# The first sample's inputs modulated in PSUM in a hybrid encoder, with new numbers for its order of work

## The chip, the cores and the metric

The kernel runs on one core of a Trainium2 chip. The metric is the device time of one execution in microseconds (us), as the median of several runs. A profile is taken in one further execution; its time is given beside its span, which goes from the first to the last instruction.

## What is computed

Two sequences of 1024 rows and 1024 columns, each with a conditioning vector, go through two layers with shared weights. For a layer:

```python
shift, scale, gate = jnp.split(jax.nn.silu(c) @ ada_w + ada_b, 3, axis=-1)
h = rmsnorm(x, norm_pre) * (1.0 + scale) + shift
u = h @ w_in                                  # 1024 x 2304
y_pool = pool_mixer(u[..., :256], ...)        # four windows
y_attn = gqa_attention(u[..., 256:1024], ...) # q, k, v; 8 heads of 64, 2 for k and v
y_rg = rglru_mixer(u[..., 1024:1280], ...)    # convolution, two linear recurrences
y = concatenate([y_pool, y_attn, y_rg]) * silu(u[..., 1280:])
x = x + gate * rmsnorm(y @ w_out, norm_post)
```

All inputs are fp32. To keep that precision the kernel splits each operand of a large product into two fp16 halves, hi and lo = value - hi, and adds up three products: hi*hi, hi*lo and lo*hi.

## The kernel before

There are four units of work, called samples 0 to 3: sample 0 is the prompt in layer 0, sample 1 the other sequence in layer 0, samples 2 and 3 the same in layer 1. Each has a stage that makes the transposed input hT (hi and lo, in two halves j of 512 rows and eight slices k of 128 columns), projections for k and v and for q, a side stream of chunks (recurrence, gate, pooling), attention in 64 units of 128 queries of one head, and the output projection (wout) in eight tiles of 128 rows.

At the beginning the modulation has to be computed as well: blocks of ada_w (adaw) are loaded, 24 in all, of which the first 16 give shift and scale; from these come the columns hgb that hT is multiplied with and shifted by. Sample 0's inputs (xt, eight blocks of 128 rows) are loaded and scaled by their row factor rs (norm, L849), four of them are transposed together per slice into a PSUM bank (turn, L862), and the result goes to xT in SBUF. If hgb is known by then, this eviction modulates; if not, it copies, and modulate (L885) does it later. modulate then writes hi, and lo is subtracted on DVE or POOL (sub_any). For samples 1 to 3 hprep_gen (L911) does the same with the bank itself as the buffer: modulate in place, copy to hi, subtract on DVE, free the bank.

The order of the instructions is not written by hand. A planner (class Order) keeps many streams of work, each of which says what it needs next: an engine, tiles, free slots of the pool of 39, PSUM banks. At each step it takes the stream that can go first by its own estimates, and among those that can go at the same time the one with the lowest rank. `soonest` puts an operation on the engine that would end it first. Every engine and the queue of DMA issues (SP) then run their lists in that order, so an instruction waits for all that stand before it on its engine.

The numbers come from four dictionaries TUNE (one a sample), START and LAYER: ranks (a stream of sample n has the rank 100 n plus its number), how far ahead of an engine a stream may be placed (P, A, D, G, S, X), how many PSUM banks may be held singly (nb) and in pairs (np), how many slots are left free by a stream (spare, qkeep, wkeep), how many tiles of wout take the eight inputs y one by one (f_major), from which chunk the next layer's w_out is prepared (wfrom). START["x"] says after how many adaw blocks the two halves of xt may be loaded; the adaw stream itself has the rank -97 (start_gen), these loads START["xr"], that is -53.8 and 1.4. TUNE[0]["h"] is the rank of h_gen for sample 0, which only starts h0_gen with START["h"].

Of the kernel before, what the change touches and what calls it, by code (L numbers as in the profile page):

```python
# [12 lines left out]
AF = mybir.ActivationFunctionType  # L13
# [3 lines left out]
P = 128  # L17
# [10 lines left out]


TUNE = [  # L30
    dict(h=-9.8, tab=-61.5, rgw=-62.8, qw=11.3, q=39.5, main=39.6, v=-93.1, rgt=6.2, attn=13.3,
         wprep=16.5, wo=39.7, side=108.5, gate=1.45, ysc=107.7, ysp=100.7, w=68.8, work=8, ds=3, nfly=8,
         s0=4, pace=(4, 61), wos=8, deep=3, f_major=5, spare=0, qkeep=1, wkeep=7, wokeep=0, slack=2.19,
         hslack=2.0, margin=0.33, P=0.6, A=1.22, D=1.02, G=1.25, S=1.3, X=2.99, nb=4, np=2, wopen=3,
         spill=2, sslack=0.0),
    dict(h=-88.0, tab=-138.2, rgw=-45.0, qw=-61.2, q=-181.1, main=65.6, v=-122.9, rgt=23.6, attn=-14.4,
         wprep=107.1, wo=85.3, side=97.8, gate=1.86, ysc=66.7, ysp=108.8, w=79.4, work=8, ds=2, nfly=5,
         s0=0, pace=(14, 64), wos=10, deep=3, f_major=6, spare=1, qkeep=5, wkeep=2, wokeep=9, slack=3.75,
         hslack=3.82, margin=0, P=0.07, A=1.29, D=0.36, G=1.39, S=1.66, X=1.74, nb=4, np=3, wopen=4,
         spill=2, sslack=0.0),  # L40
    dict(h=-56.5, tab=-120.9, rgw=-43.7, qw=-41.0, q=-17.5, main=-3.7, v=-95.2, rgt=51.8, attn=-16.0,
         wprep=71.4, wo=90.7, side=118.4, gate=0.1, ysc=142.5, ysp=110.2, w=62.9, work=6, ds=2, nfly=6,
         s0=3, pace=(15, 38), wos=9, deep=2, f_major=1, spare=4, qkeep=2, wkeep=0, wokeep=1, slack=2.33,
         hslack=2.48, margin=0.36, P=2.36, A=1.02, D=0.83, G=0.625, S=0.35, X=1.72, nb=6, np=2, wopen=3,
         spill=2, sslack=0),
    dict(h=-38.8, tab=-7.4, rgw=44.8, qw=-59.1, q=43.0, main=31.5, v=86.0, rgt=62.7, attn=36.1,
         wprep=226.9, wo=-31.1, side=118.1, gate=0.51, ysc=119.3, ysp=81.6, w=57.1, work=10, ds=3, nfly=5,
         s0=5, pace=(0, 64), wos=9, deep=4, f_major=3, spare=1, qkeep=5, wkeep=1, wokeep=0, slack=2.26,
         hslack=2.98, margin=0.87, P=0.28, A=0.15, D=0.45, G=0.9, S=1.99, X=0, nb=4, np=3, wopen=4,
         spill=2, sslack=0.28),  # L50
]
START = dict(x=(6, 16), xr=(-53.8009657012761, 1.4378218455368525), h=11.7, qw=-116.3, qw2=-141.6, qwa=9,
             prt=7, crow=4, prow=2, ada=95.9, keep=0)
LAYER = [
    dict(fly=6, keep=3, wfly=4, wfrom=(0, 0), wrank=15.7, ada=-17.0, akeep=5),
    dict(fly=3, keep=2, wfly=1, wfrom=(1, 1), wrank=163.6, ada=69.7, akeep=8),
]
LAT = {
    "P": dict(P=0.0, A=0.197, D=0.196, G=0.2, S=0.2), "A": dict(P=0.06, A=0.14, D=0.14, G=0.06, S=0.14),
# [253 lines left out]
def tile_hymba_encoder(  # L313
# [515 lines left out]
    def h0_gen(rank):  # L829
# [19 lines left out]
        def norm(j, xs, t):  # L849
            ss, rs = small(1, "ss"), small(1, "rs")  # L850
            yield need("A", [xs[t]])
            act(junk, xs[t], AF.Square, accum=ss)
            yield need("G", [ss])
            ts(rs, ss, 1.0 / D, EPS, ALU.mult, ALU.add, "G")
            tt(rs, rs, neghalf[:, :1], ALU.pow, "G")
            yield need("D", [rs])
            ts(xs[t], xs[t], rs, None, ALU.mult)
            done[j] = done.get(j, 0) + 1
            if done[j] == 4:
                yield from turn(j, xs)  # L860

        def turn(j, xs):  # L862
# [3 lines left out]
            for k in range(NK):  # L866
# [3 lines left out]
                    tp(ps[:, t * P:(t + 1) * P], xs[t][:, k * P:(k + 1) * P], ident)  # L870
                yield need("A|D", [ps])
                if ("hgb", 0) in G:
                    done["h", j, k] = True
                    g, b = (G["hgb", 0][:, i, k, 0:1] for i in range(2))
                    if soonest(("D", 0.66), ("A", 0.66)) == "D":
                        ts(xT[j, k], ps, g, b, ALU.mult, ALU.add)
                    else:
                        act(xT[j, k], ps, AF.Identity, scale=g, bias=b)
                else:
                    copy_any(xT[j, k], ps)  # L880
                free(ps)
                spawn(rank - 0.1 + 0.01 * k, modulate(j, k))
            free(*xs)

        def modulate(j, k):  # L885
            x = xT[j, k]
            hi, lo = hT(0, j, k)
            yield need("A|D", lambda: [x, G["hgb", 0]], cond=lambda: ("hgb", 0) in G)
            if ("h", j, k) in done:
                copy_any(hi, x)  # L890
            else:
                g, b = (G["hgb", 0][:, i, k, 0:1] for i in range(2))
                if soonest(("D", 0.46), ("A", 0.7)) == "D":
                    ts(hi, x, g, b, ALU.mult, ALU.add)
                else:
                    act(hi, x, AF.Identity, scale=g, bias=b)
                yield need("D", [x])
                ts(x, x, g, b, ALU.mult, ALU.add)
            yield need("D|G", [x, hi])
            sub_any(lo, x, hi, TUNE[0]["hslack"])  # L900
            G["hk", 0, j, k] = od.mark(f"hk0_{j}_{k}", hi, lo)
            done["m", j] = done.get(("m", j), 0) + 1
            if done["m", j] == 8:
                free(*xT[j])

        spawn(-99.9, columns(0))
        spawn(START["xr"][0], load(0))
# [920 lines left out]
```

## Time and profile before

| | |
|---|---|
| median of 3 runs | 1880.79 us (1875.88 to 1883.11) |
| profiled execution | 1876.88 us, its span 1875.1 us |
| matmul engine (PE) busy | 91% of the span |
| VectorE (DVE), ScalarE (ACT), GpSimd (POOL) busy | 68%, 61%, 41% |
| granted clock of TensorE, mean | 0.975 of full speed |

The page gives the busy time of each engine, the chain of work that ended last, and the costliest groups of instructions. In a group's name the written tile stands left of the arrow and the read ones right of it; L423 and the like are lines of the kernel, often of a helper (L395 issues all matrix products, L410 all of ACT's operations, L423 all of tensor_tensor). In the waits, "PE psum <- POOL hT" means that the matmul engine stood still until POOL had written hT.

### The profile page before, as it was taken

To read this page: it belongs to the slowest core of one execution; us is meant where nothing else is said; L and a number is where in the kernel's file an instruction comes from. 1 tells how busy PE (TensorE), PEld (TensorE's weight loads), DVE (VectorE), ACT (ScalarE), POOL (GpSimd) and SP (SyncE) were. 2 spreads that over 40 slices of the span, in tenths; PEclk is the share of its full clock that TensorE was granted. 3 is DMA by queue.
4 is the path that set the end of the run, shared out by engine and by line. 5 is a ranking of instruction groups with operands and counts; after the bars stand their busy time and mean duration, and the time that the engine had idled before them with its cause. 6 is when DMAs were issued, how large, how long until landed. Compare 5 with 4: busy or idle time off the path is not lost.

```text
span 1875.1 us, 35819 instructions
## 1 busy us (share of the span) xinstructions
PE 1712.4 (91%) x14267; PEld 990.7 (53%) x14267; DVE 1280.2 (68%) x2327; ACT 1140.2 (61%) x1767; POOL 760.5 (41%) x602
## 2 busy tenths in 40 slices
PE   5799899988999989999799998898789999999898
PEld 2564555544555546555456646455445755555543
DVE  4796987786345889567646689886843577866741
ACT  3665677776415667677642376678753256888721
POOL 2731452353431244234343226346643214655432
PEclk7899999999999989999899999999999999999999
DMA  9674499999365559999843446799984322999943
GB/s 345 201 208 153 99 191 233 178 214 252 136 225 191 131 137 206 168 194 214 232 147 135 101 102 128 145 251 191 179 234 151 102 68 41 178 201 195 198 133 116
DMA packets 672592, 323.58 MB, mean 173 GB/s; under 512 B 597880, under 2 KB 628776, under 8 KB 672424
## 3 DMA queue, kind: packets, MB, share of 16 engines
q1 hardware_dynamic: 672424, 321.29, 74.1%
q8 instruction: 111, 1.82, 0.4%
q14 instruction: 57, 0.47, 0.1%
HBM read 128.28 MB, written 46.15 MB: 93 GB/s over the span
## 4 chain that ended last, share of the span: by engine, by line
PE 32%; DVE 11%; issue 5%; ACT 4%; DMA 4%; POOL 4%; SPq 1%; POOLq 0%; ACTq 0%; DVEq 0%
PE psum L395 31%; POOL hh L423 4%; DMA pT<-hh 3%; DVE mx L459 3%; ACT p L410 2%; DVE psum L423 1%; ACT hh L410 1%; PE psum L403 1%; DVE y L450 1%; DMA xt<-xmid 1%; DVE sq L423 1%; SPq L479 1%; DVE hh L423 1%; DVE pdf L450 0%; DVE qss L459 0%
## 5 line engine op out<-in xcount | busy, mean ns | idle before, releaser
L423 POOL TENSOR_TENSOR hh<-p,hh 128x1024 f16<-128x1024 f32 x187 | 406.8, 2179 | 416.2 <-ACT hh L410 382.2
L395 PE MATMUL psum<-hT,w 128*128 128x512 f16 x2304 | 538.0, 381 | 5.8 <-ACT w L410 3.4
L459 DVE TENSOR_REDUCE mx<-psum 128x1 f32<-128x1024 f32 x256 | 312.0, 1219 | 94.2 <-PE psum L395 76.0
L395 PEld LDWEIGHTS <-w 128*128 128x128 f16 x2304 | 221.7, 99 | 273.6 <-issue 26.9
L395 PE MATMUL psum<-wo,y 128*128 128x512 f16 x1536 | 346.6, 382 | 3.7 <-DVE y L442 1.6
L395 PE MATMUL psum<-qkT,qkT 128*128 128x512 f16 x1024 | 265.7, 385 | 39.3 <-ACT p L410 24.7
L410 ACT ACTIVATE p<-psum,mx,qksc 128x1024 f32<-128x1024 f32 x187 | 224.1, 1199 | 106.8 <-DVE mx L444 63.9
L395 PE MATMUL psum<-w,hT 128*128 128x256 f16 x2304 | 273.5, 276 | 9.0 <-POOL hT L423 6.4
L395 PEld LDWEIGHTS <-pT 128*128 128x128 f16 x6144 | 212.8, 99 | 122.7 <-DMA pT<-hh 85.1
L395 PE MATMUL psum<-v,pT 128*128 128x64 f16 x6144 | 225.8, 194 | 54.8 <-DMA pT<-hh 54.6
L395 PEld LDWEIGHTS <-hT 128*128 128x128 f16 x2304 | 226.5, 100 | 60.3 <-issue 17.5
L395 PEld LDWEIGHTS <-y 128*128 128x128 f16 x1536 | 149.5, 99 | 175.4 <-issue 5.6
L410 ACT ACTIVATE hh<-p 128x1024 f16<-128x1024 f32 x187 | 196.5, 1053 | 4.9
L395 PEld LDWEIGHTS <-qkT 128*128 128x128 f16 x1024 | 93.0, 99 | 133.7 <-issue 58.0
L450 DVE SCALAR_TENSOR_TENSOR ot<-psum,ors,gp 128x512 f32<-128x512 f32 x64 | 45.1, 745 | 154.8 <-POOL ors L423 154.8
L410 ACT ACTIVATE junk<-psum 128x512 bf16<-128x512 f32 x64 | 38.2, 596 | 181.8 <-PE psum L395 170.4
L423 DVE TENSOR_TENSOR hh<-psum,hh 128x1024 f16<-128x1024 f32 x69 | 84.1, 1218 | 31.7 <-ACT hh L410 31.5
L423 POOL TENSOR_TENSOR ws<-ws,neghalf 128x1 f32<-128x1 f32 x46 | 28.5, 635 | 186.5 <-DVE ws L442 185.6
L423 POOL TENSOR_TENSOR ot<-ot,xres 128x1024 f32<-128x1024 f32 x31 | 73.2, 2361 | 66.7 <-DVE ot L450 32.5
L410 ACT ACTIVATE psum<-psum,mx,qksc 128x1024 f32<-128x1024 f32 x69 | 80.8, 1170 | 24.1 <-DVE mx L444 19.4
L410 ACT ACTIVATE hh<-psum 128x1024 f16<-128x1024 f32 x69 | 70.3, 1019 | 1.7
L423 POOL TENSOR_TENSOR qrs<-qrs,neghalf 128x8 f32<-128x8 f32 (+1 forms) x48 | 68.7, 1432 | 4.0
(219 smaller groups left out, 2073.1 us busy)
## 6 DMA issues: line engine op xcount, KB each, us to landing
adaw<-in_ada_w_dram SPq DMA_DIRECT2D x48, 512.0 KB, 6.1
wraw<-in_w_in_dram SPq DMA_DIRECT2D x36, 512.0 KB, 6.4
wd<-w SPq DMA_DIRECT2D x36, 512.0 KB, 3.3
w<-wd SPq DMA_DIRECT2D x36, 512.0 KB, 4.7
wo<-wd SPq DMA_DIRECT2D x32, 512.0 KB, 6.2
woraw<-in_w_out_dram SPq DMA_DIRECT2D x16, 512.0 KB, 4.6
wd<-wo SPq DMA_DIRECT2D x16, 512.0 KB, 4.1
xmid<-ot SPq DMA_DIRECT2D x16, 512.0 KB
```

What stands on the lines that cost most here:

```text
L395: nc.tensor.matmul(out[:, :m], lhsT, rhs, start=start and i == 0, stop=stop and i == len(pairs) - 1)
L403: nc.tensor.transpose(out, in_, idn)
L410: nc.scalar.activation(out=out, in_=in_, func=func, **kw)
L423: eng.tensor_tensor(out=out, in0=a, in1=b, op=op)
L450: nc.vector.scalar_tensor_tensor(out=out, in0=a, scalar=s, in1=b, op0=op0, op1=op1)
L459: nc.vector.tensor_reduce(out=out, in_=a, op=op, **{"axis": AX.X, **kw})
L479: nc.sync.dma_start_transpose(out=out, in_=in_)
```

## The change

Sample 0 gets the same path as the others: where hgb is known at a slice's eviction, a new stream (inplace) modulates in the bank, copies hi from it, subtracts lo on DVE and frees the bank. Slices evicted before hgb go through xT and modulate as they did. The row scaling of xt may be placed on ACT or DVE (mul_any) instead of on DVE alone. Numbers of TUNE, START and LAYER are different.

```diff
--- before.py
+++ after.py
@@ -28,32 +28,32 @@
 
 
 TUNE = [
-    dict(h=-9.8, tab=-61.5, rgw=-62.8, qw=11.3, q=39.5, main=39.6, v=-93.1, rgt=6.2, attn=13.3,
-         wprep=16.5, wo=39.7, side=108.5, gate=1.45, ysc=107.7, ysp=100.7, w=68.8, work=8, ds=3, nfly=8,
+    dict(h=-2.1, tab=-46.4, rgw=-62.8, qw=11.3, q=39.5, main=39.6, v=-93.1, rgt=6.2, attn=13.3,
+         wprep=16.5, wo=39.7, side=108.5, gate=1.45, ysc=107.7, ysp=100.7, w=50.2, work=8, ds=3, nfly=8,
          s0=4, pace=(4, 61), wos=8, deep=3, f_major=5, spare=0, qkeep=1, wkeep=7, wokeep=0, slack=2.19,
          hslack=2.0, margin=0.33, P=0.6, A=1.22, D=1.02, G=1.25, S=1.3, X=2.99, nb=4, np=2, wopen=3,
          spill=2, sslack=0.0),
-    dict(h=-88.0, tab=-138.2, rgw=-45.0, qw=-61.2, q=-181.1, main=65.6, v=-122.9, rgt=23.6, attn=-14.4,
-         wprep=107.1, wo=85.3, side=97.8, gate=1.86, ysc=66.7, ysp=108.8, w=79.4, work=8, ds=2, nfly=5,
-         s0=0, pace=(14, 64), wos=10, deep=3, f_major=6, spare=1, qkeep=5, wkeep=2, wokeep=9, slack=3.75,
-         hslack=3.82, margin=0, P=0.07, A=1.29, D=0.36, G=1.39, S=1.66, X=1.74, nb=4, np=3, wopen=4,
+    dict(h=-88.0, tab=-138.2, rgw=-45.0, qw=-61.2, q=-181.1, main=65.6, v=-111.7, rgt=23.6, attn=-14.8,
+         wprep=107.1, wo=88.3, side=97.8, gate=1.86, ysc=66.7, ysp=114.6, w=79.4, work=8, ds=2, nfly=5,
+         s0=0, pace=(14, 64), wos=10, deep=3, f_major=6, spare=3, qkeep=5, wkeep=2, wokeep=9, slack=3.75,
+         hslack=3.82, margin=0, P=0.07, A=1.29, D=0.36, G=1.39, S=1.16, X=1.74, nb=4, np=3, wopen=4,
          spill=2, sslack=0.0),
-    dict(h=-56.5, tab=-120.9, rgw=-43.7, qw=-41.0, q=-17.5, main=-3.7, v=-95.2, rgt=51.8, attn=-16.0,
+    dict(h=-56.5, tab=-108.9, rgw=-43.7, qw=-41.0, q=-17.5, main=21.1, v=-95.2, rgt=51.8, attn=-16.0,
          wprep=71.4, wo=90.7, side=118.4, gate=0.1, ysc=142.5, ysp=110.2, w=62.9, work=6, ds=2, nfly=6,
-         s0=3, pace=(15, 38), wos=9, deep=2, f_major=1, spare=4, qkeep=2, wkeep=0, wokeep=1, slack=2.33,
-         hslack=2.48, margin=0.36, P=2.36, A=1.02, D=0.83, G=0.625, S=0.35, X=1.72, nb=6, np=2, wopen=3,
+         s0=3, pace=(15, 38), wos=9, deep=2, f_major=3, spare=4, qkeep=2, wkeep=0, wokeep=1, slack=2.33,
+         hslack=2.48, margin=0.36, P=2.36, A=1.02, D=0.83, G=0.47, S=0.35, X=1.72, nb=5, np=2, wopen=3,
          spill=2, sslack=0),
     dict(h=-38.8, tab=-7.4, rgw=44.8, qw=-59.1, q=43.0, main=31.5, v=86.0, rgt=62.7, attn=36.1,
-         wprep=226.9, wo=-31.1, side=118.1, gate=0.51, ysc=119.3, ysp=81.6, w=57.1, work=10, ds=3, nfly=5,
-         s0=5, pace=(0, 64), wos=9, deep=4, f_major=3, spare=1, qkeep=5, wkeep=1, wokeep=0, slack=2.26,
+         wprep=231.8, wo=-31.1, side=118.1, gate=0.51, ysc=119.3, ysp=81.6, w=57.1, work=10, ds=3, nfly=5,
+         s0=5, pace=(0, 64), wos=9, deep=4, f_major=7, spare=1, qkeep=5, wkeep=3, wokeep=0, slack=2.26,
          hslack=2.98, margin=0.87, P=0.28, A=0.15, D=0.45, G=0.9, S=1.99, X=0, nb=4, np=3, wopen=4,
-         spill=2, sslack=0.28),
+         spill=2, sslack=0.37),
 ]
-START = dict(x=(6, 16), xr=(-53.8009657012761, 1.4378218455368525), h=11.7, qw=-116.3, qw2=-141.6, qwa=9,
+START = dict(x=(3, 14), xr=(-53.8009657012761, 1.4378218455368525), h=11.7, qw=-116.3, qw2=-118.9, qwa=9,
              prt=7, crow=4, prow=2, ada=95.9, keep=0)
 LAYER = [
-    dict(fly=6, keep=3, wfly=4, wfrom=(0, 0), wrank=15.7, ada=-17.0, akeep=5),
-    dict(fly=3, keep=2, wfly=1, wfrom=(1, 1), wrank=163.6, ada=69.7, akeep=8),
+    dict(fly=6, keep=3, wfly=4, wfrom=(0, 0), wrank=15.7, ada=-30.2, akeep=5),
+    dict(fly=3, keep=2, wfly=1, wfrom=(1, 3), wrank=163.6, ada=71.7, akeep=8),
 ]
 LAT = {
     "P": dict(P=0.0, A=0.197, D=0.196, G=0.2, S=0.2), "A": dict(P=0.06, A=0.14, D=0.14, G=0.06, S=0.14),
@@ -853,8 +853,8 @@
             yield need("G", [ss])
             ts(rs, ss, 1.0 / D, EPS, ALU.mult, ALU.add, "G")
             tt(rs, rs, neghalf[:, :1], ALU.pow, "G")
-            yield need("D", [rs])
-            ts(xs[t], xs[t], rs, None, ALU.mult)
+            yield need("A|D", [rs])
+            mul_any(xs[t], xs[t], rs)
             done[j] = done.get(j, 0) + 1
             if done[j] == 4:
                 yield from turn(j, xs)
@@ -870,38 +870,51 @@
                     tp(ps[:, t * P:(t + 1) * P], xs[t][:, k * P:(k + 1) * P], ident)
                 yield need("A|D", [ps])
                 if ("hgb", 0) in G:
-                    done["h", j, k] = True
-                    g, b = (G["hgb", 0][:, i, k, 0:1] for i in range(2))
-                    if soonest(("D", 0.66), ("A", 0.66)) == "D":
-                        ts(xT[j, k], ps, g, b, ALU.mult, ALU.add)
-                    else:
-                        act(xT[j, k], ps, AF.Identity, scale=g, bias=b)
-                else:
-                    copy_any(xT[j, k], ps)
+                    spawn(rank - 0.1 + 0.01 * k, inplace(j, k, ps))
+                    continue
+                copy_any(xT[j, k], ps)
                 free(ps)
                 spawn(rank - 0.1 + 0.01 * k, modulate(j, k))
             free(*xs)
+
+        def inplace(j, k, ps):
+
+            g, b = (G["hgb", 0][:, i, k, 0:1] for i in range(2))
+            if soonest(("D", 0.72), ("A", 0.66)) == "D":
+                ts(ps, ps, g, b, ALU.mult, ALU.add)
+            else:
+                act(ps, ps, AF.Identity, scale=g, bias=b)
+            hi, lo = hT(0, j, k)
+            yield need("A|D", [ps])
+            if soonest(("D", 0.6), ("A", 0.48)) == "D":
+                copy(hi, ps)
+            else:
+                act(hi, ps, AF.Copy)
+            yield need("D", [ps, hi])
+            tt(lo, ps, hi, ALU.subtract)
+            free(ps)
+            over(j, k, hi, lo)
+
+        def over(j, k, hi, lo):
+            G["hk", 0, j, k] = od.mark(f"hk0_{j}_{k}", hi, lo)
+            done["m", j] = done.get(("m", j), 0) + 1
+            if done["m", j] == 8:
+                free(*xT[j])
 
         def modulate(j, k):
             x = xT[j, k]
             hi, lo = hT(0, j, k)
             yield need("A|D", lambda: [x, G["hgb", 0]], cond=lambda: ("hgb", 0) in G)
-            if ("h", j, k) in done:
-                copy_any(hi, x)
+            g, b = (G["hgb", 0][:, i, k, 0:1] for i in range(2))
+            if soonest(("D", 0.46), ("A", 0.7)) == "D":
+                ts(hi, x, g, b, ALU.mult, ALU.add)
             else:
-                g, b = (G["hgb", 0][:, i, k, 0:1] for i in range(2))
-                if soonest(("D", 0.46), ("A", 0.7)) == "D":
-                    ts(hi, x, g, b, ALU.mult, ALU.add)
-                else:
-                    act(hi, x, AF.Identity, scale=g, bias=b)
-                yield need("D", [x])
-                ts(x, x, g, b, ALU.mult, ALU.add)
+                act(hi, x, AF.Identity, scale=g, bias=b)
+            yield need("D", [x])
+            ts(x, x, g, b, ALU.mult, ALU.add)
             yield need("D|G", [x, hi])
             sub_any(lo, x, hi, TUNE[0]["hslack"])
-            G["hk", 0, j, k] = od.mark(f"hk0_{j}_{k}", hi, lo)
-            done["m", j] = done.get(("m", j), 0) + 1
-            if done["m", j] == 8:
-                free(*xT[j])
+            over(j, k, hi, lo)
 
         spawn(-99.9, columns(0))
         spawn(START["xr"][0], load(0))
```

## Rows read from the trace of the kernel before

**Rows 1.** Page, busy time: us (share of the span) x instructions, the matmul engine.

```profile
PE 1712.4 (91%) x14267; PEld 990.7 (53%) x14267; DVE 1280.2 (68%) x2327; ACT 1140.2 (61%) x1767; POOL 760.5 (41%) x602
```

**Rows 2.** Stretches: start:end, length, busy us (x instructions) of each engine, PEclk, DMA share, GB/s.

```profile
0.00:100.00 100.00, 63.98 (x389) 41.87 (x390) 60.05 (x189) 55.29 (x100) 48.85 (x65) 0.80 0.79 270
1300.00:1325.00 25.00, 17.13 (x257) 10.55 (x255) 21.51 (x33) 22.99 (x34) 17.67 (x10) 0.96 1.12 198
```

**Rows 3.** Waits of the matmul engine, 47 to 100 us: total, times, longest, all us.

```profile
PE psum L395 <- POOL hT L423: 6.4, 8, 1.4
```

**Rows 4.** Timeline to 75 us: start, us, engine, line, operation, count [idle before <-releaser].

```profile
17.32 4.65 SPq L471 DMA_DIRECT2D adaw<-in_ada_w_dram  x6
22.96 3.04 SPq L471 DMA_DIRECT2D xt<-in_x_prompt_dram  x4
...
45.76 0.78 ACT L410 ACTIVATE xT<-psum,hgb 128x512 f32<-128x512 f32 x1 [0.62 <-DVE hgb L442]
49.41 8.88 POOL L423 TENSOR_TENSOR hT<-xT,hT 128x512 f16<-128x512 f32 x7 [0.36 <-DVE xT L444]
...
54.74 0.62 ACT L410 ACTIVATE hT<-xT 128x512 f16<-128x512 f32 x1
55.02 1.08 DVE L551 TENSOR_SCALAR gm<-gm 128x2 int32<-128x2 int32 x1
...
59.19 0.15 DVE L551 TENSOR_SCALAR ws<-ws 128x1 int32<-128x1 int32 x1 [0.66 <-POOL ws L423]
...
65.87 0.19 POOL L444 TENSOR_SCALAR rs<-ss 128x1 f32<-128x1 f32 x1
...
67.91 0.78 ACT L410 ACTIVATE xT<-psum,hgb 128x512 f32<-128x512 f32 x1 [5.01 <-PE psum L403]
```

**Rows 5.** Groups on tile hT, 0 to 130 us: durations ns min/median/max, first and last start.

```profile
L423 POOL TENSOR_TENSOR hT<-xT,hT x16: 1147/1158/2142, 47.9 to 80.6; 128x512 f16<-128x512 f32 x16
...
L410 ACT ACTIVATE hT<-xT,hgb x4: 798/800/802, 46.4 to 48.6; 128x512 f16<-128x512 f32 x4
L455 DVE CAST hT<-xT x3: 710/735/1377, 49.7 to 75.5; 128x512 f16<-128x512 f32 x3
```

**Rows 6.** Groups on tile hT, 1370 to 1430 us, when the last sample's are made.

```profile
L423 DVE TENSOR_TENSOR hT<-psum,hT x16: 676/682/692, 1400.8 to 1422.7; 128x512 f16<-128x512 f32 x16
L410 ACT ACTIVATE hT<-psum x14: 592/597/611, 1399.7 to 1422.1; 128x512 f16<-128x512 f32 x14
```

**Rows 7.** Timeline, 73 to 104 us.

```profile
73.50 8.20 POOL L423 TENSOR_TENSOR hT<-xT,hT 128x512 f16<-128x512 f32 x7
73.73 8.05 SPq L471 DMA_DIRECT2D wraw<-in_w_in_dram  x4
...
77.04 1.22 ACT L410 ACTIVATE hT<-xT 128x512 f16<-128x512 f32 x2
...
97.29 2.52 PE L395 MATMUL psum<-hT,w 128*128 128x512 f16 x6 [0.44 <-DVE ws L551]
```

**Rows 8.** Stretches between 66 and 100 us.

```profile
66.00:82.00 16.00, 10.08 (x73) 7.09 (x72) 10.14 (x29) 13.87 (x27) 13.76 (x15) 0.95 0.75 253
82.00:94.00 12.00, 11.99 (x89) 9.96 (x89) 10.84 (x40) 8.47 (x17) 5.43 (x9) 0.78 1.04 319
94.00:100.00 6.00, 3.09 (x11) 1.68 (x12) 5.83 (x22) 5.61 (x11) 2.50 (x4) 0.79 0.76 227
```

**Rows 9.** Groups on tile xt, 420 to 960 us, the row scaling.

```profile
L442 DVE TENSOR_SCALAR xt<-xt,rs x9: 745/754/1417, 464.9 to 925.2; 128x1024 f32<-128x1024 f32 x9
...
L410 ACT ACTIVATE xt<-xt,rs x7: 1132/1133/1155, 426.8 to 921.5; 128x1024 f32<-128x1024 f32 x7
```

**Rows 10.** Groups by line and shape, 900 to 1400 us: busy, mean ns, idle before.

```profile
L395 PE MATMUL psum<-wo,y 128*128 128x512 f16 x540 | 124.0, 385 | 2.5 <-DVE y L442 1.6 <-ACT p L410 0.6 <-DVE y L450 0.3
...
L395 PE MATMUL psum<-qkT,qkT 128*128 128x512 f16 x256 | 67.4, 387 | 18.5 <-ACT p L410 12.9 <-DVE rt L467 2.1 <-DVE ru L423 2.0
...
L410 ACT ACTIVATE gth<-psum,wu 128x512 f32<-128x512 f32 x16 | 10.8, 677 | 4.4 <-PE psum L395 4.4
```

## The prediction before the run

> **What bounds the kernel now.** I first read the busy shares of the page [rows 1]: the matmul engine is busy 1712.4 of 1875.1 us, and every other engine is well below it. So time can come only from the 163 us in which it is idle and from what it loses at the lower clock. Next come the stretches [rows 2]: of the first 100 us it works 64.0. The start therefore holds 36 of the 163 idle us, and it is the part that the code change touches; the edited numbers touch the rest.
>
> Inside the start, the list of what the matmul engine waited for [rows 3] names the low halves of hT, made on POOL, first: 6.4 us in 8 waits between 47 and 100 us. The timeline [rows 4] shows why. The loads of the first sample's rows (xt) are issued at 22.96 us, behind the last of the 16 blocks of adaw (six issued from 17.32), and the first eviction that uses the modulation columns hgb starts at 45.76. From 47.9 POOL makes eight low halves [rows 5], the last seven from 49.41 in 8.88 us (1.27 each), to 58.29. Meanwhile DVE is held up: an operation on two elements takes 1.08 us at 55.02, while one on a single element takes 0.15 at 59.19, when POOL makes no low half. Then POOL builds the rotary tables, and only after them, at 65.87, the row factor of the eighth xt, for which the second half's transposes wait. The second half runs from its first eviction (67.91) to its last low half (73.50+8.20 = 81.70 [rows 7]): 13.8 us.
>
> **The change part by part.**
>
> *Low halves from POOL to DVE.* All 16 are on POOL now, 1.15 us or more each [rows 5]. A slice whose columns hgb are there at its eviction is now modulated in PSUM, copied to hi and subtracted on DVE. That is what samples 1 to 3 do, and there the subtraction took 0.682 us, the copy 0.597 on ACT [rows 6]. The first four slices of half one were evicted before hgb, as the four hi copies that still apply hgb show [rows 5], so I take 12 slices for the new path and 4 for the old; the bounds are 8 and 16. POOL loses 12 x 1.27 = 15 us, DVE gains 12 x 0.682 = 8.2 us. DVE gets some of it back where POOL no longer holds it up, 0.93 us (1.08-0.15) in each such place; with two of them it carries about 6 us more.
>
> *First half.* POOL's four remaining low halves end at 47.9+4x1.27 = 53.0 instead of 58.3: 5.3 us is the upper bound. The lower one is 0: ACT is full there, from its first eviction at 45.76 until the hi copy of 54.74 ends at 55.36, and with one subtraction behind it (0.68) the last slice is ready at 56.0, which alone gives 2.3. I take the middle of 2.3 and 5.3, rounded down to 3.5 us. The tables on POOL and the row factor behind them move with it, so the second half starts 3.5 us earlier too; this is the same gain and is counted once.
>
> *Second half.* The nearest rows are the 16 slices of sample 3 made in the same way: the first low half at 1400.8, the last at 1422.7, so 1.46 us a slice [rows 6]. Eight slices take 7 x 1.46 plus the three passes of the last (0.78+0.60+0.68), 12.3 us, against 13.8: 1.5 us. If ACT alone sets it, its last hi copy ends at 78.26 [rows 7], and 0.68 later, at 78.9, the half is ready: 2.8 us. I take 2. A slice now holds its PSUM bank for three passes instead of one; with four single banks, some of them held by the projection, that is why I don't take more.
>
> *Clock.* From 66 to 82 the matmul engine works 10.08 of 16 us, and from 82 to 94, when it works 11.99 of 12, the granted clock is 0.78 [rows 8], a mixture of the two levels 1.2 and 2.4 GHz. If the work before is denser, part of these 12 x 0.22 = 2.6 us comes back. Bounds 0 and 2.6, taken 1.5.
>
> *What is late next.* At 97.29 the first chunk of the recurrence starts [rows 7]; the engine works 3.09 of the 6 us from 94 [rows 8]. Its weights' loads are issued from 73.73, among the second half's work, as slots come free; if they don't move, what was gained before is idle time there. That is a rival below.
>
> *Row scaling to ACT.* DVE needs 0.75 for a row block and ACT 1.13 (the same form in samples 1 and 2) [rows 9]. In half one this lies before hgb at 45.7, which waits for the adaw blocks, so it costs nothing; without that cover at most 4 x 0.38 = 1.5 us.
>
> *START.* The new counts x=(3, 14) let the loads become eligible after 3 and 14 adaw blocks instead of 6 and 16. But the adaw stream has rank -97, the loads -53.8 and 1.4, and of streams that may go at the same time the lower rank goes: with 6 allowed they went after 16. I cost it at nothing; if they did go earlier, four loads would push hgb back by about the 3.04 us of their issue. TUNE[0]["h"] ranks only a stub, and LAYER[0]["ada"] is read nowhere.
>
> *Sample 2.* Over 900 to 1400 us the scores waited 12.9 us for ACT to release their PSUM pairs, the projections out 2.5 us, mostly for y [rows 10]. With nb=5 one bank less can be held singly, so a second pair is more often possible; f_major=3 lets three tiles instead of one use y as it arrives. I take a third of 12.9, that is 4 us, for the first (bounds 12.9 gained and the loss below) and 1 for the second (0 to 2.5).
>
> *The other numbers* (spare, wfrom, S, wkeep, sslack, ranks) reorder work that is beside the matmul engine, in either direction for all that the rows show. I take 0, with 8 us either way as an estimate: the idle time of one bad stretch, the 25 us from 1300 with 7.87 idle [rows 2].
>
> *Sum:* 3.5+2+1.5+4+1 = 12 us. The profiled execution took 1876.9 us (span 1875.1), so 1864.9. It lies 3.9 us below the median of the runs, 1880.8; on that basis the forecast is 1869.
>
> **A rule that speaks against it.** A DVE copy to hi from xT in SBUF took 0.71 us or more, the subtraction that reads PSUM 0.682 for as many elements [rows 5, 6]: no loss by the rows, though the copies from SBUF ran while POOL was busy. The Trainium skill ("VectorE: DVE Perf Modes", section "Why PSUM operands drop a tier") says that fp32 operands in PSUM hold DVE to one element a cycle, while an SBUF copy may run at twice that. By that rule a DVE copy to hi would cost about 0.35 us more in PSUM, an estimate from that page, and 12 of them 4 us.
>
> **The rivals.**
> - *The recurrence's weights set the end of the start.* For it: the engine is idle half of the time from 94 to 100 [rows 8], the chunk comes at 97.29, and the loads of these weights are queued behind others on SP. Against it: they wait for slots that the second half frees. Then the start gives 0 to 3 us and the rest 5: 1874, within 0.5%.
> - *DVE becomes the bound of the start.* For it: it works 5.83 of the 6 us from 94 and 10.84 of the 12 before [rows 8], so 6 us more of it may come out at the end. Against it: it has 5.9 of the 16 us from 66 free. The start's 7 shrinks to 1, and with sample 2's 5 the time is 1875, again within 0.5%.
> - *Slower: sample 2 lacks the bank.* Its projections write 36 banks of results (12 chunks in two halves, and three groups of q and kv in four parts). If each comes one eviction later, 0.677 us by the gate's row [rows 10], that is 24 us; with the start's 7 gained the time is 1898. It decides where the engine has nothing else to do, as in the 25 us from 1300 with 7.87 idle [rows 2]. Against it: the limit of 5 differs from 6 only while at most one pair is taken.
> - *The edit does less than it says:* if hgb comes after most evictions in the new order, 8 or fewer slices take the new path and the start gives 3 us: 1873.
>
> **How the numbers follow.** I give my forecast, with all that is faster still, 0.54, the two rivals within the start 0.2 together, the smaller edit 0.12 and the slower one 0.14. A run of this kernel can tell about 0.5%, 9.4 us, from no change; the forecast at -12 is just past it, so some 0.02 of it falls inside, with the rivals at 1873 to 1875. Faster 0.52, same 0.34, slower 0.14. The range goes from 1853 (the start's bounds 5.3, 2.8 and 2.6, half of the 12.9, 2.5 for y and the 8 of the other numbers: 28 us) to 1890 (half-way from the median to the slower case, and a little more).
>
> **What would show it.** In the new profile POOL should make about 4 of the low halves and DVE 12; the list of waits should have less than 3 us for POOL hT; the second half's eighth row factor should be near 62 instead of 65.87, the first chunk of the recurrence near 91 instead of 97.29; the scores of sample 2 should wait about 9 us for ACT. The prediction is wrong if that chunk stays at 97, or if sample 2's projections show new waits for banks.

## The result, and the profile after

The changed kernel takes 1903.88 us (median of 4 runs, 1903.43 to 1908.59); the kernel before, on the same chip, 1878.34. The ratio is 1.0142 with a 95% interval of 1.0108 to 1.0176: slower by some 25 us, where I forecast 12 faster. The profiled execution took 1904.0 us, its span is 1902.3, the mean granted clock 0.962 instead of 0.975.

The page's busy row of after ("answers [rows 1]" means the same view as in that group, now of after):

```profile
PE 1737.0 (91%) x14267; PEld 1000.4 (53%) x14267; DVE 1296.0 (68%) x2333; ACT 1146.7 (60%) x1770; POOL 764.9 (40%) x597
```

The same matmuls are busy 24.6 us longer, and the engine's idle time is 165.3 us (1902.3 less 1737.0) instead of 162.7. So this profile gives most of the loss to matmuls that run longer, that is, to the clock. One profile isn't enough for that split, as the experiments show.

The start has the operations that the change says. Loads, and groups on tile hT from 0 to 130 us (answers [rows 4, 5]):

```profile
17.46 4.68 SPq L471 DMA_DIRECT2D adaw<-in_ada_w_dram  x6
23.13 3.04 SPq L471 DMA_DIRECT2D xt<-in_x_prompt_dram  x4
```

```profile
L423 DVE TENSOR_TENSOR hT<-psum,hT x12: 676/682/692, 52.8 to 82.5; 128x512 f16<-128x512 f32 x12
L423 POOL TENSOR_TENSOR hT<-xT,hT x4: 1147/1359/1387, 49.5 to 53.9; 128x512 f16<-128x512 f32 x4
L455 DVE CAST hT<-psum x4: 680/686/692, 54.6 to 81.8; 128x512 f16<-128x512 f32 x4
```

Twelve low halves are on DVE and four on POOL, at the predicted 0.682 us. The waits of the matmul engine from 38 to 100 us (answers [rows 3]):

```profile
PE psum L395 <- DVE hT L423: 3.6, 4, 1.6
PE psum L395 <- ACT junk L410: 3.5, 1, 3.5
PE psum L395 <- POOL hT L423: 2.7, 2, 1.4
```

POOL's 6.4 us became 2.7, and a new wait for DVE's hT took the 3.6 in its place. The timeline shows the second half (answers [rows 7]):

```profile
62.90 0.19 POOL L444 TENSOR_SCALAR rs<-ss 128x1 f32<-128x1 f32 x1
...
66.40 0.75 ACT L410 ACTIVATE psum<-psum,hgb 128x512 f32<-128x512 f32 x1 [2.03 <-PE psum L403]
...
73.77 1.06 PE L403 MATMUL psum<-ident,xt 128*128 128x128 f32 x4
75.40 0.68 DVE L423 TENSOR_TENSOR hT<-psum,hT 128x512 f16<-128x512 f32 x1
...
76.33 1.06 PE L403 MATMUL psum<-ident,xt 128*128 128x128 f32 x4
77.85 0.68 DVE L423 TENSOR_TENSOR hT<-psum,hT 128x512 f16<-128x512 f32 x1
...
78.77 1.06 PE L403 MATMUL psum<-ident,xt 128*128 128x128 f32 x4
...
82.47 0.69 DVE L423 TENSOR_TENSOR hT<-psum,hT 128x512 f16<-128x512 f32 x1
...
99.78 1.44 PE L395 MATMUL psum<-hT,w 128*128 128x512 f16 x3 [1.21 <-DVE ws L551]
```

The eighth row factor comes at 62.90 instead of 65.87. But the half then takes 16.8 us, from 66.40 to 83.16, instead of 13.8: from 73 us the slices go one at a time, a transpose every 2.5 us, each after the subtraction of an earlier slice. The first chunk of the recurrence is at 99.78 instead of 97.29. That difference needs care: the moment at which DVE has written hgb moves from profile to profile. The end of its last operation on hgb, in before (44.53+1.13 = 45.66) and in after (46.70):

```profile
44.53 1.13 DVE L442 TENSOR_SCALAR hgb<-mod,sh 128x16 f32<-128x16 f32 x1
```

```profile
46.47 0.23 DVE L442 TENSOR_SCALAR hgb<-mod,sh 128x16 f32<-128x16 f32 x1
```

In five kernels below whose start is unedited hgb comes at 44.58 to 48.02 and the chunk at 96.16 to 99.29, always 51.3 to 52.2 us after it. Counted from hgb, the chunk comes 53.1 us later in after and 51.6 in before, so the start costs about 1.5 us, and all the rest of the loss arises later. Of the stretches (answers [rows 8]), the first is the second half:

```profile
66.00:84.00 18.00, 12.85 (x73) 8.35 (x72) 14.79 (x37) 13.83 (x26) 3.13 (x5) 0.70 0.82 285
84.00:96.00 12.00, 10.47 (x87) 9.10 (x84) 10.90 (x40) 9.43 (x19) 5.48 (x8) 0.88 0.97 296
```

The same two stretches have a clock of 0.90 and 0.86 in before, and 0.81 to 0.93 in the five kernels with the start unedited. So the second half's 0.70 is low, and the 0.88 behind it says nothing. Sample 2, which I expected to gain, from 920 to 1420 us (answers [rows 10]):

```profile
L395 PE MATMUL psum<-wo,y 128*128 128x512 f16 x537 | 124.0, 388 | 3.6 <-DVE ot L450 1.6 <-ACT p L410 1.3 <-DVE hT L423 0.7
L395 PE MATMUL psum<-qkT,qkT 128*128 128x512 f16 x256 | 68.2, 391 | 20.7 <-ACT p L410 17.3 <-DVE ws L442 1.6 <-DVE sg L450 0.9
```

Its scores wait 17.3 us for ACT instead of 12.9. How a later loss looks, in the stretch in which sample 0's output projection runs, of after and then of before:

```profile
460.00:560.00 100.00, 94.54 (x536) 50.72 (x535) 34.56 (x75) 37.23 (x77) 31.45 (x42) 0.95 0.51 175
```

```profile
440.00:540.00 100.00, 98.06 (x612) 53.59 (x611) 39.14 (x81) 39.44 (x77) 27.93 (x41) 1.00 0.58 187
```

Before has the engine full at full clock; after has 3.5 us more idle and a clock of 0.95. After, the last result of attention (pv) in sample 0 ends at 482.2 us, and the clock falls for 10 us from 483; before, it ends at 450.0. The later attention matmuls stand between the output projection's in another order.

### The profile page after: what moved, and what is told of

Its sections match the earlier page's. It is cut to its first block, busy times and chain, and to the rows that moved or that the text cites. A ratio compares the mean times of both kernels' runs of the same rounds, so it can differ in the third digit from the quotient of the medians.

```text
span 1902.3 us, 35860 instructions
## 1 busy us (share of the span) xinstructions
PE 1737.0 (91%) x14267; PEld 1000.4 (53%) x14267; DVE 1296.0 (68%) x2333; ACT 1146.7 (60%) x1770; POOL 764.9 (40%) x597
## 5 line engine op out<-in xcount | busy, mean ns | idle before, releaser
L423 POOL TENSOR_TENSOR hh<-p,hh 128x1024 f16<-128x1024 f32 x190 | 412.5, 2173 | 409.1 <-ACT hh L410 363.5
L395 PEld LDWEIGHTS <-w 128*128 128x128 f16 x2304 | 221.7, 99 | 270.9 <-issue 30.2
L395 PE MATMUL psum<-qkT,qkT 128*128 128x512 f16 x1024 | 272.4, 393 | 39.5 <-ACT p L410 27.5
L444 POOL TENSOR_SCALAR qrs<-qss,wu 128x8 f32<-128x8 f32 (+1 forms) x48 | 13.1, 273 | 162.0 <-DVE qss L459 160.7
```

The costliest lines, as they stand in the source:

```text
L395: nc.tensor.matmul(out[:, :m], lhsT, rhs, start=start and i == 0, stop=stop and i == len(pairs) - 1)
L423: eng.tensor_tensor(out=out, in0=a, in1=b, op=op)
L444: eng.tensor_scalar(out=out, in0=a, scalar1=s1, scalar2=s2, op0=op0, op1=op1)
```

## The experiments

**The measure.** In a re-laid kernel the path and the order of everything else change together. I therefore compared, engine by engine, the sequence of instructions with the kernel before. The matmul engine's list has 27,301 places; "11742, from 97" means that so many hold another instruction than before, the first at 97. Instructions are told apart by the names of the tiles that they write and read, not by the part of a tile, so the numbers are on the low side. The table has for each run the ratio to the kernel before, the unlike places, and of the profiled execution: the matmul engine's idle time, its busy time at the lower level of the clock (1.2 GHz, by the trace's record of the granted clock), and how much later than before the last wout matmul of samples 0 to 3 ended (us).

| run | median us | ratio (95%) | unlike | idle | at 1.2 GHz | later, samples 0 to 3 |
|---|---|---|---|---|---|---|
| before | 1877.5 to 1880.6 | | | 162.7 | 67.6 | |
| after | 1903.88 | 1.0142 (1.0108 to 1.0176) | 11742, from 97 | 165.3 | 116.8 | 21.9, 30.0, 25.5, 27.2 |
| e1_code | 1907.67 | 1.0146 (1.0109 to 1.0184) | 12654, from 97 | 172.5 | 101.1 | 22.8, 32.3, 23.9, 30.2 |
| e2_numbers | 1908.54 | 1.0143 (1.0119 to 1.0166) | 8339, from 7543 | 170.7 | 114.5 | 2.3, 19.5, 33.7, 32.0 |
| e3_rowscale | 1911.59 | 1.0164 (1.0139 to 1.0189) | 10999, from 97 | 174.2 | 110.5 | 2.8, 14.6, 34.0, 32.0 |
| e4_inplace | 1906.54 | 1.0137 (1.0113 to 1.0161) | 12842, from 224 | 174.0 | 91.6 | 16.5, 20.4, 26.9, 28.5 |
| e5_figure20 | 1905.42 | 1.0140 (1.0123 to 1.0157) | 12752, from 334 | 173.7 | 105.4 | -1.0, 11.9, 31.5, 29.0 |
| e6_figure100 | 1907.48 | 1.0157 (1.0142 to 1.0172) | 12632, from 97 | 171.5 | 101.2 | 9.2, 27.8, 29.7, 28.9 |
| e15_figure_less20 | 1892.60 | 1.0072 (1.0054 to 1.0091) | 12653, from 334 | 167.8 | 87.4 | 2.4, 11.9, 13.3, 16.3 |
| e16_figure_less100 | 1924.34 | 1.0236 (1.0219 to 1.0253) | 12842, from 158 | 186.9 | 115.9 | 16.8, 27.2, 47.0, 43.8 |
| e17_figure_act | 1893.16 | 1.0072 (1.0055 to 1.0089) | 12283, from 334 | 167.6 | 86.0 | -0.9, 21.4, 13.0, 17.5 |
| e12_layer | 1890.22 | 1.0062 (1.0048 to 1.0076) | 7741, from 7543 | 159.0 | 99.7 | -0.1, 14.2, 15.0, 12.5 |
| e7_tune2 | 1888.79 | 1.0057 (1.0040 to 1.0074) | 5376, from 12915 | 163.1 | 82.4 | -0.2, 2.5, 4.2, 8.6 |
| e13_figure_s1 | 1881.89 | 1.0020 (1.0007 to 1.0032) | 5045, from 6032 | 161.6 | 77.5 | 0.2, 2.2, 6.8, 6.4 |
| e14_figure_s2 | 1876.96 | 1.0002 (0.9992 to 1.0012) | 231, from 13131 | 157.6 | 70.1 | 0.4, 0.9, -0.3, -0.6 |
| e8_held_path | 1882.50 | 1.0022 (1.0008 to 1.0037) | 0 | 165.5 | 74.5 | 4.3, 5.6, 6.2, 5.9 |
| e9_held_lo | 1877.74 | 0.9997 (0.9986 to 1.0009) | 0 | 154.2 | 78.3 | -2.2, -4.9, -4.0, -4.2 |
| e10_held_odd | 1877.92 | 0.9996 (0.9983 to 1.0008) | 0 | 154.1 | 106.3 | 3.1, 1.9, 5.9, 5.9 |
| e11_held_first | 1879.01 | 1.0002 (0.9990 to 1.0014) | 0 | 153.2 | 89.2 | 1.2, 0.1, 0.1, -0.6 |

**Which part of the change.** All hunks of code without the numbers (e1), the numbers without the code (e2), the new path alone (e4: inplace, over and modulate), and the row scaling alone (e3):

```diff
-            yield need("D", [rs])
-            ts(xs[t], xs[t], rs, None, ALU.mult)
+            yield need("A|D", [rs])
+            mul_any(xs[t], xs[t], rs)
```

> The code of the change (inplace, row scaling on ACT or DVE) with every number of the kernel before. Theory 1, the code alone lays sample 0 out worse: the output projection of sample 0 ends about 22 us later than before (533 to 555 in the changed kernel), little is added after it, and the time is 1895 to 1905. Theory 2, the numbers of samples 1 to 3 cost the time: 1870 to 1883.

> The code before with every number of the change. START and TUNE[0] leave the order of all instructions as it was, so sample 0 should end within 1 us of before by either theory. Theory 1: what is left are the +8 us of sample 1 and the -4.5 of sample 2 seen in the changed kernel, if they come from the numbers: 1875 to 1888. Theory 2: 1895 or more.

> Before, with the row scaling of the first sample allowed on ACT or DVE and nothing else. Theory 1 in the form that the bank held through three passes is what costs: within 5 us of before, 1873 to 1884. Rival, any edit at the start lays the whole rest out anew, and the rest decides: a shift of 8 us or more in either direction that arises after 100 us.

> Before, with the inplace path alone; the row scaling stays on DVE. Theory 1 by the held bank: like the code as a whole, 1893 to 1905, with the second half's preparation 16 to 17 us long as in the changed kernel (13.8 before). Rival, the new order of the rest decides: the second half is again 16 to 17 us, but the end differs from the code as a whole by 8 us or more.

Each of the four loses as much as all together, 26 to 31 us, so the parts don't add up. e1 ends sample 0 22.8 us later, as its theory 1 had it, but 7 us more are added after that, and its time lies above the 1905 given. e4's lies there too and fits neither of its theories: its second half takes 17.8 us, yet its first chunk comes 52.0 us after hgb, as with the start unedited, and its time is within 1.2 us of e1's. In e2 the new START and TUNE[0] change nothing: its order is new only in sample 1, and its loss begins there. Even the row scaling, eight operations at the start, brings 31, of which its profile has only 2.8 by the end of sample 0. What the parts have in common is that each re-lays the order of much that follows.

**No part of it.** Two placebos leave work and numbers alone; the planner only believes DVE busy for 0.02 (e5) or 0.10 us (e6) longer after each of sample 0's row scalings:

```diff
-            ts(xs[t], xs[t], rs, None, ALU.mult)
+            ts(xs[t], xs[t], rs, None, ALU.mult); od.free_at["D"] += 0.02
```

> Before, with nothing of the work edited: after each of the first sample's eight row scalings the planner's own clock for DVE is put 0.02 us later, an edit to its bookkeeping alone. From place 334 of 27301 on, the order on the matmul engine comes out new. Theory 1 (the new path is what costs; a new order by itself costs nothing on average): 1874 to 1888. Rival, the order of before was an unusually good one and any other costs about what the four runs so far did: 1895 to 1912.

> The same with 0.10 us instead of 0.02, so another new order from place 97 on. Theory 1: 1874 to 1888, or a scatter to both sides of before over the two runs. Rival: 1895 to 1912 again, with the loss in other stages than in the run with 0.02.

They lose 26 and 30 us, inside the rival's range. The new order alone is enough. e5's busy row and its clock in 40 slices of the span, with the clock of before beneath:

```profile
PE 1730.3 (91%) x14267; PEld 1002.0 (53%) x14267; DVE 1267.6 (67%) x2332; ACT 1138.6 (60%) x1760; POOL 781.1 (41%) x609
PEclk8899999999999989999899999899899999999999
```

```profile
PEclk7899999999999989999899999999999999999999
```

There is no one place to point at: the loss is spread over samples 1 and 2 (11.9 us later after sample 1, 31.5 after sample 2), partly as idle time and partly as a lower clock.

**Only from a later sample on.** e7 has only TUNE[2]'s new numbers (the order is new from place 12915, where sample 1's output projection begins, and sample 2 beside it), e12 only LAYER's (new from place 7543, in sample 1). e13 and e14 are placebos there:

```diff
-            mul_any(xs[t], xs[t], rs)
+            mul_any(xs[t], xs[t], rs); od.free_at["D"] += 0.3 * (n == 1)
```

and in e14 `0.1 * (n == 2)`; e7's numbers are those of the third dict of the change, e12's those of LAYER.

> Before, with the change's numbers of TUNE[2] alone (main, f_major, G, nb, tab). The order is that of before up to place 12915 of the matmul engine, the start of sample 2, and new behind it. If the numbers themselves are better, as the prediction had it: 1870 to 1878 (4 and 1 us gained). If a new order costs, but only from where it begins: the first two samples end as before (998 us within 2) and the whole takes 1886 to 1900.

> Only the edited numbers of LAYER (from which chunk on the next layer's w_out is prepared). The order on the matmul engine is new from place 7543 of 27301, in the second unit of work; all before it stays. If a new order costs wherever it begins, and the more the longer the re-laid rest: between the run with only sample 2's numbers (+11 us) and those re-laid from the start (+27 us), so 1889 to 1905, with nothing lost in the first sample. If only the order of the start matters: within 5 us of before.

> No work and no number edited: the planner counts 0.3 us more for each row scaling of the second unit of work (sample 1), which puts 5045 of the matmul engine's 27301 places in another order, the first at 6032. If any re-laid order costs, in step with how much of it is new: the placebos from the start had 12,600 to 12,750 unlike places and lost 27 to 29 us, so some 11 us, 1886 to 1894, none of it in sample 0. If the loss of the late orders came from the edited numbers: within 4 us of before.

> No work and no number edited: the planner counts 0.1 us more for each row scaling of the third unit of work (sample 2); 231 places of the matmul engine are in another order, 867 of DVE's, 547 of ACT's. If the cost goes with the unlike places of the matmul engine: under 1 us, 1876 to 1881. If any disturbance of the order costs, however small: 5 us or more.

In none is anything lost ahead of the place where the order is new. e7 and e12 lose 11 and 12 us, as expected, e13 4 (I had expected 11 from its unlike places), e14 nothing. Less new order costs less here, but not in step with the unlike places: e2, with 8339, lost 27.

**The other direction.** The line of e5 with `+= -0.02` (e15) and `+= -0.1` (e16), and with ACT's clock, `od.free_at["A"] += 0.1` (e17).

> No work edited: the planner counts 0.02 us less for each row scaling of sample 0 instead of more; 12653 places of the matmul engine are in another order. If the loss comes from booking DVE later: this goes the other way, 1860 to 1880. If any order re-laid from the start loses against before's: 1895 to 1912, as the seven so far (1904 to 1912).

> No work edited: 0.10 us less for each row scaling of sample 0; 12842 places. By the direction of the figure: 1855 to 1880. By leaving before's order: 1895 to 1912.

> No work edited: the planner counts ACT, not DVE, as 0.10 us longer busy after each row scaling of sample 0, which hands work from ACT to DVE; 12283 places. By the direction of the figure: within 10 us of before. By leaving before's order: 1895 to 1912.

They lose 13, 44 and 13 us. A loss through DVE being booked later falls with that: with the figure moved the other way it is the largest of all (e16) and the smallest (e15). The other expectation held in the sign alone: 1892.6, 1893.2 and 1924.3 lie on both sides of the 1895 to 1912 that I gave. That seven orders agreed within 8 us was chance. Ten new orders (after, e1 to e6, e15 to e17) cost 13 to 44 us, and none gained.

**The path with the order held.** Here the planner books the old operations, so that the matmul engine's and the loads' sequences are unlike in no place, while the new ones are issued. e8 has the whole path of sample 0; e11 only its first half; in e9 the twelve slices still go through xT, only their low halves are subtracted on DVE; e10 does that for every second of the sixteen slices. The core of e8, where od.op is the booking, and of e9 (which books the old subtraction behind it):

```diff
-                        act(xT[j, k], ps, AF.Identity, scale=g, bias=b)
+                        nc.scalar.activation(out=ps, in_=ps, func=AF.Identity, scale=g, bias=b)
+                        od.op("A", 0.051 + 512 * 0.000833 + 0.186, [xT[j, k]], [ps, g, b])
+                    nc.scalar.activation(out=hi, in_=ps, func=AF.Copy)
+                    nc.vector.tensor_tensor(out=lo, in0=ps, in1=hi, op=ALU.subtract)
...
-            sub_any(lo, x, hi, TUNE[0]["hslack"])
+            if ("h", j, k) in done:
+                e = soonest(("D", 0.00104 * 512), ("G", 0.0022 * 512, TUNE[0]["hslack"]))
+                nc.vector.tensor_tensor(out=lo, in0=x, in1=hi, op=ALU.subtract)
```

In e10 the condition of e9 is `k % 2`, in e11 that of e8 has `and j == 0`.

> Before, with the new path's work in the first sample and the order of everything else held: where hgb is known the slice is modulated in its bank, copied to hi on ACT and subtracted on DVE, all at the place of the old eviction, while the planner books the old operations; matmul engine and DMA queue keep their order in every place. Theory 1, the path itself costs (bank held, DVE loaded): 1893 or more. Rival, only the order costs: 1870 to 1885, since POOL's low halves no longer hold the start.

> Only one effect of the new path, with the order of the matmul engine and of the loads as before: in the first sample the low halves of the slices that were modulated at their eviction are subtracted on DVE, from xT in SBUF, at the place in the order where POOL did it; a slice still frees its PSUM bank after one pass. Theory A (relieving POOL gains, as I predicted 3.5 + 2 us; what ate it in the held path was the bank kept for three passes): 4 to 7 us faster than before, 1871 to 1876. Theory B (the wait for POOL was not the one that set the start; another comes in its place): within 3 us of before, and the first chunk of the recurrence stays within 1 us of 97.3. Theory C (DVE becomes the bound): 3 or more us slower.

> As the run with all low halves on DVE, but only every second slice's: DVE and POOL share them. Theory A: most of the gain, 3 to 6 us, since each engine has half. Theory B: within 3 us of before. Theory C: about half the loss of the other run, 1 to 3 us slower.

> The held path (modulated in PSUM, split from there, order of the matmul engine and of the loads as before) for the first half's slices alone; the second half goes through xT as before. If the loss of 4 us of the held path comes from the second half's banks, which the transposes wait for beside the running projections: no slower than before, 1874 to 1879. If it comes from the path in either half: 2 to 4 us slower than before.

The whole path costs 4 us (1.5 to 7), its first half nothing that can be measured (2 us faster to 2.6 slower). Only four of the twelve slices are in the first half, so these times alone would not part the halves; the first chunk does. Counted from hgb, it is late in e8 and in no other held run, so the second half costs it:

| run | hgb written | second half takes | first chunk | chunk after hgb |
|---|---|---|---|---|
| before | 45.66 | 13.8 | 97.29 | 51.6 |
| e2, e7, e12, e13, e14 (start unedited) | 44.58 to 48.02 | 13.8 | 96.16 to 99.29 | 51.3 to 52.2 |
| e8_held_path | 47.51 | 14.6 | 102.79 | 55.3 |
| e11_held_first | 45.69 | 12.9 | 97.34 | 51.7 |
| e9_held_lo | 44.81 | 13.0 | 96.57 | 51.8 |
| e10_held_odd | 46.42 | 12.2 | 97.92 | 51.5 |
| after | 46.70 | 16.8 | 99.78 | 53.1 |

(The new operations stand where the planner had none, so 4 us is the path's price in this order, not in the best one for it.) e8's waits from 38 to 100 us, and its timeline:

```profile
PE psum L403 <- DVE hT L883: 6.7, 3, 2.6
PE psum L395 <- POOL hT L423: 2.8, 3, 1.4
```

```profile
72.48 0.68 DVE L883 TENSOR_TENSOR hT<-psum,hT 128x512 f16<-128x512 f32 x1
73.22 1.09 PE L403 MATMUL psum<-ident,xt 128*128 128x128 f32 x8 [2.09 <-DVE hT L883]
...
76.39 1.97 PE L403 MATMUL psum<-ident,xt 128*128 128x128 f32 x8 [2.08 <-DVE hT L883]
...
102.79 2.57 PE L395 MATMUL psum<-hT,w 128*128 128x512 f16 x6 [0.44 <-DVE ws L551]
```

The transposes (L403) wait for a subtraction on DVE, which is what frees a bank now: 6.7 us, and in the held order the projection's matmuls stand behind them. The first chunk comes 5.5 us later than in before's profile; 1.9 of that was there when hgb came, ahead of the edit, and 3.6 belong to the path, near the 4 us of the times.

With the banks freed after one pass (e9) that wait is gone, and the work of POOL is on DVE all the same. Its waits, its group and its first chunk:

```profile
PE psum L395 <- ACT hT L410: 3.2, 2, 2.9
PE psum L395 <- POOL hT L423: 3.1, 3, 1.4
PE psum L395 <- DVE hT L902: 2.3, 3, 1.1
```

```profile
L902 DVE TENSOR_TENSOR hT<-xT,hT x12: 680/682/1635, 51.7 to 78.9; 128x512 f16<-128x512 f32 x12
```

```profile
77.66 1.89 DVE L902 TENSOR_TENSOR hT<-xT,hT 128x512 f16<-128x512 f32 x3
...
96.57 2.45 PE L395 MATMUL psum<-hT,w 128*128 128x512 f16 x6 [0.44 <-DVE ws L551]
```

POOL's wait is halved, and ACT's and DVE's hT take its place: 8.6 us for hT together. The second half takes 0.8 us less than before, yet from hgb the chunk comes no sooner. (In the profile it is 0.72 us earlier than before's, but hgb was 0.85 earlier.) What e9 gained by the second half's start, 0.5 us counted from hgb, ACT loses again at 72.72, where it waits for DVE, which has the subtractions now. Behind the half the matmul engine's list has sums of squares of w_out (wsq), for which it waits for ACT (junk). ACT starts them at 77.34, 32.5 us after hgb; in before it is at 78.08, 32.4 after it. Three lines of e9, then two of before:

```profile
72.72 0.66 ACT L410 ACTIVATE ks<-psum 128x256 f16<-128x256 f32 x2 [0.46 <-DVE psum L423]
...
77.34 1.09 ACT L410 ACTIVATE junk<-woraw 128x1024 bf16<-128x1024 f32 x1
...
78.57 0.59 PE L395 MATMUL psum<-wsq,ones 128*128 128x1 f32 x2 [1.05 <-ACT junk L410]
```

```profile
78.08 1.12 ACT L410 ACTIVATE junk<-woraw 128x1024 bf16<-128x1024 f32 x1
...
79.35 0.38 PE L395 MATMUL psum<-wsq,ones 128*128 128x1 f32 x2 [0.64 <-ACT junk L410]
```

The chunk itself starts when DVE has made the low half of its weights (in e9 at 96.45, in before at 97.17); the ws that its line names ends beside its start. e9 and e10 differ from before by less than 1 us, with intervals from 3 us faster to 2 slower: theory B held. In before's order the 3.5 and 2 us that I counted at the start don't come from relieving POOL.

**Idle or clock.** The ten new orders have a mean idle time of 172.4 us and 103.0 us of matmul at 1.2 GHz; the six with before's order of the matmul engine in all but 231 places (before, e8 to e11, e14) have 157.9 and 81.0. Work at 1.2 GHz takes twice as long (matmuls of 512 columns that follow one another start 427 ns apart there and 216 at full clock, medians in before), so half of the 22.0 is lost: 14.5 + 11.0 = 25.5 of the 27.4 us between their mean spans (1903.6 and 1876.2). The granted clock of all runs agrees: 0.971 in the mean of 75 runs of before, 0.957 to 0.970 in the ten new orders. The split says where the time is, not why the clock was lower. A single profile doesn't give it: with one and the same order, e9 and e10 have equal idle time and 78.3 and 106.3 us at 1.2 GHz, and spans 10 us apart.

What stays open is which property of before's order is lost. The loss does not begin in the same sample in all runs, and I found no wait that all share. One rival explanation needs no such property: before's numbers look like the outcome of a search (START["xr"] is given to thirteen decimals and more), and if it is the best of many orders, most others are worse. No run here tests that. No re-laid order beat before, and of the held ones none did by more than can be measured, so there is no better version to give.

## Why the prediction was wrong

- *The step that failed* is this: "reorder work that is beside the matmul engine, in either direction for all that the rows show. I take 0, with 8 us either way". The order does not stay beside the matmul engine: it is the order of that engine too, in 11,742 of 27,301 places. The term measured 27 us in e2, the numbers alone, and 13 to 44 us over the ten new orders, never a gain. The estimate of 8 came from the idle time of one stretch; about half of the loss is idle time in small pieces, most of the other half clock, and neither is in such a row. That a new order costs is shown; by what mechanism is open.
- *The same error hid in the code edits.* I gave each a local price, and none for what it does to the planner. The row scaling "costs nothing" where it stands, and e3 lost 31 us with it.
- *First half, 3.5 us:* POOL's waits fell as forecast (2.7, under 3), the row factor came at 62.90 (near 62), and counted from hgb the second half began 2.5 us sooner. But the chunk was at 99.78, not near 91, which I had named as the sign of being wrong: the second half, 3.0 us longer, lost that again. In the held order (e9) the relief is worth nothing at the chunk: the wait moves to ACT's and DVE's hT, and behind it stand ACT's squares for w_out and the weights' low half on DVE. That is part of the first rival, and with DVE busy 14.8 of 18 us in after also of the second; these runs don't separate the two.
- *Second half, 2 us:* 16.8 us instead of 12.3. I took the distance of slices from sample 3 [rows 6] and saw that a bank is held for three passes, but gave it no price. Sample 3's transposes waited for DVE's hT once, 2.1 us (before, 1395 to 1425); e8's waited 6.7 in three waits. That the projection's banks make the difference is likely and not shown. e8 less e11 gives the price, about 4 us (3.7, uncertain by 3.5), and the chunk's 3.6 agrees.
- *Clock, 1.5 us:* behind the second half, from 82 to 94, the clock is 0.80 instead of 0.78, and with the start unedited it is anything from 0.73 to 0.91 there. So the 0.78 that I built on was one draw of a scatter, no gain is shown, and the second half itself fell to 0.70.
- *Sample 2, 5 us:* the scores' wait for ACT went from 12.9 to 17.3 instead of 9. With TUNE[2] alone (e7) it was this:

```profile
L395 PE MATMUL psum<-qkT,qkT 128*128 128x512 f16 x256 | 68.1, 390 | 16.5 <-ACT p L410 13.1 <-DVE ws L442 1.6 <-DVE sg L450 0.9
```

  13.1, so no gain from the bank, and 11 us lost all the same.
- *The slower rival* had the sign and nearly the time (1898), by another mechanism: in after the output projections of sample 2 waited 3.6 instead of 2.5 us, not 24. That nearness is luck.
- *What was right:* twelve and four low halves, 0.682 us each, START and TUNE[0]["h"] at nothing (the loads stand where they stood), the row factor, POOL's wait. That POOL held DVE up is confirmed as well: the operation on two elements that took 1.08 us takes 0.17 in e9, where POOL makes nothing at that time:

```profile
55.17 0.17 DVE L551 TENSOR_SCALAR gm<-gm 128x2 int32<-128x2 int32 x1
```

## What to carry to other kernels

Where a planner lays out the whole program, an edit has two prices: its own, which rows can give, and that of a new order for everything after it, which no row gives. Measure the second with a placebo that moves one figure of the planner and no work, and the first with the order held, before a local gain of a few us is believed or blamed. And before an engine is relieved, look for what is ready next behind it: in e9 a half that took 0.8 us less was worth nothing at the next chunk. Count such differences from an event ahead of the edit: with the start unedited, one and the same chunk scattered over 3 us, and over 1 us when counted from hgb.

## What the runs showed of the hardware

The price of reading PSUM, which the rows of before couldn't show, came out in e9, where POOL makes no low half beside the later copies. DVE's copy to hi from xT in SBUF, in e9 (timeline):

```profile
48.82 2.69 POOL L423 TENSOR_TENSOR hT<-xT,hT 128x512 f16<-128x512 f32 x2 [0.36 <-DVE xT L444]
49.12 1.38 DVE L455 CAST hT<-xT 128x512 f16<-128x512 f32 x1
...
74.46 0.42 DVE L455 CAST hT<-xT 128x512 f16<-128x512 f32 x1
76.06 0.42 DVE L455 CAST hT<-xT 128x512 f16<-128x512 f32 x1
```

With POOL idle it takes 0.42 us; from PSUM it takes 0.68 in after; beside a low half on POOL (48.82 to 51.5) it takes 1.38. So the rule of the Trainium skill ("VectorE: DVE Perf Modes", section "Why PSUM operands drop a tier") holds here, with 0.27 us for each of after's four DVE copies, 1.1 us in all, where I had estimated 0.35 for each of twelve; in [rows 5] POOL's work had hidden it. The subtraction takes 0.68 from either.
